# Sparse attention with a per-query search for the top 256 keys: visits of four key blocks, shorter search steps tied in order, and a memory pool of their own for selections and search buffers

## The chip, the cores and the metric

One Trainium2 chip, one of its cores. The metric is the time of the whole program on the device, in microseconds (us), as a median of runs. PE is TensorE (matmuls; its weight loads are shown as PEld), DVE is VectorE, ACT is ScalarE, POOL is GpSimd, SP is SyncE, which issues the DMAs.

## What is computed

One decoder layer on a prompt of 2048 tokens (and one new token for each of eight sequences with a cache of 4096 keys). The input projection feeds two groups of heads. One is RWKV-7 time mixing, a recurrence over the tokens. The other is sparse attention: an indexer scores every earlier key of a query, the 256 best keys are selected, and softmax attention runs over these alone. Both outputs go through one output projection.

```
s = relu(einsum('bqhd,bsd->bqhs', qi, kidx))          # 8 indexer heads
score = einsum('bqhs,bqh->bqs', s, wi)
score = where(arange(L)[None, :] <= qpos[:, None], score, -inf)
_, sel = top_k(score, 256)
k_sel, v_sel = gather_kv(sel)
logits = einsum('bqgrd,bqkgd->bqgrk', qg, k_sel) * HEAD_DIM ** -0.5   # 2 kv heads, 4 q heads each
p = softmax(where(valid, logits, -inf))
o = einsum('bqgrk,bqkgd->bqgrd', p, v_sel)
...
mix = concatenate([att, rw_out], -1) @ w_out
y = x + gate * mix
```

## The kernel before

The program has two phases. The first (`phase_g`) makes all projections and the RWKV heads. Its memory lies in pools stacked one behind the other on the left side of on-chip memory: `hp` holds the normalised input `h` (65,536 bytes per partition), `wp` four weight buffers `w` of 8,192 bytes and a staging buffer `wst` of 4,096, `bs` constants, and `bu` and `bv` the work buffers of the RWKV chunks, among them three `UA` buffers of 8,192 bytes. The last chunks of RWKV (`g_tail`) run after the last projection has read `h`; they end with a small chain on DVE and ACT (a norm, L796 to L814) and two transposes on PE (L810).

The second phase (`phase_a`) is attention over the 16 blocks of 128 queries, with L = 128 (i + 1) keys for block i. Its pools are stacked over the same memory: `ac` (constants, keys `K`, values `Vn`; 43.8 KB per partition), `aq` (query tiles `qT` and `qiT`, three score buffers `sc` of 8,192 bytes, the search's columns `sm`, the ReLU buffers `r`; 43.5 KB), and `ap` (everything else: the selections `bias`, three of 4,096 bytes, the search's buffer `t1` of 8,192, the probabilities `P`, `pT`, and small tiles). The pools are made with `reuse_waits="tile"`. The pools of the background work lie above `ap`.

Every block goes through three jobs:

- `scores(i)`: for each of 8 indexer heads, PE multiplies (L1031), ACT takes the ReLU (L1048), DVE adds it with the head's weight into `sc` (L1049). 8 turns for each 1024 keys.
- `search(i)`: finds a threshold for each query that leaves 256 keys. After a start from mean and square (L1069 to L1086), six steps of a bracketing method: ACT counts the keys above the trial value with Sign and an accumulated sum (L1092), and some twenty instructions on columns of 128 x 1 make the next trial value (L1093 to L1133). They run on POOL, for blocks 4 and 5 on DVE. At the end DVE and POOL make `t1` (L1137, L1138), DVE takes the eight largest (L1141) and writes the selection `bias`, 0 or a huge negative number for each key (L1144). Sign and Square write their unused result into a part of `bias`.
- `attend(i)`: for each of 4 pairs of heads, PE makes logits (L1031), DVE adds `bias` and takes the maximum (L1262), ACT takes the exponential (L1270). Then come the visits: for two key blocks at a time PE transposes the probabilities of both heads (L1279, 4 transposes, into one of two `t` banks), ACT copies them to `pT` (L1282), and PE multiplies them with the values (L1286, 4 products on tiles of 128 x 64).

Blocks are taken in the order 4, 15, 5, 14, 6, 13, 7, 12, 8, 11, 9, 10, 3, 2. In stage s, `merge` interleaves turn by turn the search of the stage's block, the attention of the block two stages back (in stage 3 also of blocks 0 and 1) and the scores of the next block, each in proportion to its stated number of turns. Every third turn it also advances the background: the decode tokens' work and, for blocks that are done, the output projection (`outproj`, L1342). The order in which the program emits instructions isn't yet the order on the engines: a scheduler orders each engine's instructions by their priority and its own estimate of time. `later(n)` shifts the priority: searches are moved ahead by 2000, the background back by 1500. On the chip each engine runs its instructions in that fixed order. `after(a, [b])` tells the scheduler to place `a` behind `b`, without a semaphore.

## Time and profile before

| | us |
|---|---|
| median of 3 runs | 2493.24 (2489.59 to 2494.8) |
| the profiled execution | 2486.81 |
| its span, first to last instruction | 2485.0 |
| PE busy | 2151.5 (87%) |
| DVE busy | 1603.3 (65%) |
| POOL busy | 1111.7 (45%) |
| ACT busy | 1056.2 (43%) |

The profile is of one execution. Busy times of PE include the time in which a slower clock was granted, and the ends of matmuls are modelled. In the rows, a tile's name stands for all its buffers, `out<-in` says what an instruction writes and reads, x is a count, and what follows `<-` in brackets is what ended the engine's idle time before it. Projections and RWKV take the first 1400 us, attention and the rest what remains; the two overlap for some 90 us.

### The profile page before, as it was taken

What the parts mean: (1) busy time and instruction counts of PE and PEld (TensorE: products, weight loads), DVE (VectorE), ACT (ScalarE), POOL (GpSimd) and SP (SyncE); (2) the same over time, 40 slices, a digit from 0 to 9 for tenths busy, and PEclk for the clock granted to TensorE, in tenths of its full rate; (3) what the DMA queues carried; (4) which work ended last, traced back from release to release, by engine and by line L of the source; (5) the groups of instructions that cost most, each with busy time, mean ns of one, the idle gap of its engine ahead of it and who ended that gap; (6) DMA issues with size and microseconds to landing.
All of it is one profiled execution on the core that took longest, in us unless ns stands there. A gap on an engine that the chain in (4) does not pass through costs nothing.

```text
span 2485.0 us, 57674 instructions
## 1 busy us (share of the span) xinstructions
PE 2151.5 (87%) x21559; PEld 1493.0 (60%) x21559; DVE 1603.3 (65%) x5101; ACT 1056.2 (43%) x2192; POOL 1111.7 (45%) x3369
## 2 busy tenths in 40 slices
PE   6778999599999999979999664898787898899997
PEld 2546777477778777867877431354444554555554
DVE  3873477477776566667777577766787754567421
ACT  1642233233333333322233245777776652665430
POOL 2311335233424234432334216447776774787712
PEclk9889999699999999999999775999998999999999
DMA  6434333321111211112211511322000032221233
GB/s 221 147 115 113 96 96 95 83 55 41 32 46 42 55 51 40 51 40 60 54 36 32 125 35 55 100 65 64 18 18 10 18 86 77 60 59 44 65 104 95
DMA packets 268196, 167.73 MB, mean 67 GB/s; under 512 B 108647, under 2 KB 240704, under 8 KB 267777
## 3 DMA queue, kind: packets, MB, share of 16 engines
q1 hardware_dynamic: 262465, 149.26, 21.6%
q0 software_dynamic: 3328, 10.49, 1.6%
q8 instruction: 171, 2.80, 0.5%
q10 hardware_dynamic: 2112, 4.19, 0.5%
q14 instruction: 120, 0.98, 0.1%
HBM read 113.87 MB, written 50.00 MB: 66 GB/s over the span
## 4 chain that ended last, share of the span: by engine, by line
PE 41%; POOL 22%; DMA 10%; DVE 9%; issue 8%; SPq 5%; ACT 4%; POOLq 0%; DVEq 0%; ACTq 0%
PE ps_g L196 10%; PE ps_s L1342 5%; PE ps_g L204 4%; PE ps_l L1031 3%; PE ps_v L1286 3%; PE ps_t L1279 3%; POOL Ut L652 2%; POOL Us L653 2%; SPq L644 2%; PE ps_e L619 2%; PE ps_g L159 2%; POOL sm L1123 1%; SPq L655 1%; ACT bias L1092 1%; DMA TT<-tsc 1%
## 5 line engine op out<-in xcount | busy, mean ns | idle before, releaser
L196 PE MATMUL ps_g<-h,w 128*128 128x256 f16 x4032 | 503.0, 279 | 13.1 <-ACT h L439 6.3
L196 PEld LDWEIGHTS <-w 128*128 128x128 f16 x4536 | 407.6, 100 | 93.4 <-issue 13.1
L652 POOL TENSOR_TENSOR Ut<-As,Us 128x12 f32<-128x12 f32 (+10 forms) x480 | 130.5, 272 | 282.8 <-DMA As<-asc 231.9
L204 PE MATMUL ps_g<-w,h 128*128 128x256 f16 (+1 forms) x2304 | 254.0, 264 | 0.3 <-ACT nat L849 0.2
L1262 DVE CUSTOM_DVE_ANT_0 P<-ps_l,bias 128x1024 f32<-128x1024 f32 (+7 forms) x192 | 172.0, 907 | 98.2 <-PE ps_l L1031 56.3
L204 PEld LDWEIGHTS <-h 128*128 128x128 f16 x2304 | 197.7, 99 | 30.7 <-issue 3.2
L1286 PE MATMUL ps_v<-pT,Vn 128*64 128x128 f32 x2176 | 185.8, 295 | 33.5 <-ACT pT L1282 33.2
L1049 DVE SCALAR_TENSOR_TENSOR sc<-r,wi,sc 128x1024 f32<-128x1024 f32 (+7 forms) x154 | 169.2, 1099 | 66.9 <-ACT r L1048 64.8
L1282 ACT COPY pT<-ps_t 128x512 f32<-128x512 f32 (+1 forms) x288 | 153.4, 559 | 130.1 <-PE ps_t L1279 129.7
L1279 PE MATMUL ps_t<-cf,P 128*128 128x128 f32 x1088 | 188.0, 296 | 15.4 <-ACT P L1270 15.0
L1270 ACT ACTIVATE P<-P,mx 128x1024 f32<-128x1024 f32 (+7 forms) x192 | 171.3, 895 | 53.1 <-DVE mx L1268 52.7
L1286 PEld LDWEIGHTS ps_v<-pT,Vn 128*64 128x64 f32 x2176 | 119.7, 141 | 114.8 <-ACT pT L1282 58.1
L1342 PE MATMUL ps_s<-wo,mt 128*128 128x512 f16 x768 | 173.8, 382 | 11.0 <-DVE sm L1142 7.6
L1031 PE MATMUL ps_l<-K,qT 128*128 128x512 f16 (+3 forms) x640 | 151.6, 359 | 23.2 <-ACT r L1048 16.3
L1092 ACT ACTIVATE bias<-sc,sm 128x640 uint8<-128x640 f32 (+13 forms) x84 | 109.7, 1307 | 143.7 <-POOL sm L1133 128.2
L1048 ACT ACTIVATE r<-ps_l 128x1024 f32<-128x1024 f32 (+7 forms) x176 | 141.4, 814 | 67.9 <-PE ps_l L1031 37.1
L1031 PE MATMUL ps_l<-K,qiT 128*128 128x512 f16 (+3 forms) x608 | 152.6, 377 | 18.8 <-DVE mx L1262 12.0
L1279 PEld LDWEIGHTS ps_t<-cf,P 128*128 128x128 f32 x1088 | 124.6, 147 | 69.0 <-issue 39.2
L653 POOL TENSOR_TENSOR Us<-Us,Ut 128x12 f32<-128x12 f32 (+10 forms) x480 | 132.1, 275 | 34.3
L1342 PEld LDWEIGHTS <-mt 128*128 128x128 f16 x768 | 75.2, 98 | 98.9 <-issue 15.2
L1031 PEld LDWEIGHTS <-qT 128*128 128x128 f16 x640 | 62.4, 101 | 79.9 <-issue 41.6
L1031 PEld LDWEIGHTS <-qiT 128*128 128x128 f16 x608 | 59.6, 105 | 82.2 <-issue 46.7
(584 smaller groups left out, 4284.0 us busy)
## 6 DMA issues: line engine op xcount, KB each, us to landing
xt<-in_xT SPq DMA_DIRECT2D x16, 512.0 KB
wa<-in_w_ada SPq DMA_DIRECT2D x8, 1024.0 KB
kxd<-pg SPq DMA_DIRECT2D x32, 256.0 KB
qTd<-qo SPq DMA_DIRECT2D x32, 256.0 KB
kx<-kxd SPq DMA_DIRECT2D x64, 128.0 KB
mt<-mixd SPq DMA_DIRECT2D x16, 512.0 KB
x<-in_x SPq DMA_DIRECT2D x32, 256.0 KB
out_y_p<-x SPq DMA_DIRECT2D x32, 256.0 KB
```

The lines of the kernel that those rows point to most:

```text
L196: self.PE.matmul(out, w[:, a, k], h[:, b, k], start=(n == 0), stop=(n == 3 * KD - 1))
L204: self.PE.matmul(out, h[:, b, k], w[:, a, k], start=(n == 0), stop=(n == 3 * KD - 1))
L652: G.tensor_tensor(Ut[:, 0:m, j + 1:], bc(As[:, j:j + 1, j + 1:], sh), bc(Us[:, 0:m, j:j + 1], sh), op=OP.mult)
L653: G.tensor_tensor(Us[:, 0:m, j + 1:], Us[:, 0:m, j + 1:], Ut[:, 0:m, j + 1:], op=OP.add)
L1031: self.PE.matmul(ps[:, j:j + m], qs, self.K[:, kk, c0 + j:c0 + j + m], start=st, stop=not st)
L1049: V.scalar_tensor_tensor(sc[:, c:c + n], r[:, :n], wi[:, h:h + 1], self.tz[:, c:c + n] if h == 0 else sc[:, c:c + n], op0=OP.mult, op1=OP. ...
L1262: V.tensor_tensor_reduce(P[n][:, :w], pl[:, :w], bias[:, c:c + w], scale=1.0, scalar=-3.0e38, op0=OP.add, op1=OP.max, accum_out=mx[:, h, n ...
L1270: A.activation(P[n][:, :w], P[n][:, :w], AF.Exp, scale=0.125, bias=mx[:, h, 2:3], accum_out=sums[:, n, h:h + 1])
L1279: PE.transpose(pt[:, q:q + 128], Ps[g][k // 8][:, k % 8 * 128:(k % 8 + 1) * 128], self.ident)
L1282: A.copy(pT[:, :w], pt[:, :w])
L1286: PE.matmul(pv[64 * g:64 * g + 64, hh * 128:(hh + 1) * 128], self.Vn[:, k, 64 * g:64 * g + 64], pT[:, q:q + 128], start=(k == 0), stop=(k ...
L1342: PE.matmul(pg, mt[:, b, k], self.wo[:, a, k, js], start=(n == 0), stop=(n == 3 * KD - 1))
```

## The change

Three things are done together.

- A new pool `as` stands between `ac` and `aq` and takes `bias` (3 x 4,096 bytes), `t1` (8,192) and `v8` (128) out of `ap`. `qT` (3 x 2,048) moves from `aq` to `ap`, and `pT` gets a fourth buffer.
- The search keeps its bracket with the sign turned, and its steps are written with fused instructions of two operations, whose operands may be columns: 13 instructions in the first step in place of 18, 16 in the next three in place of 22, 21 in the last two in place of 31; 11 ahead of the steps in place of 13, one new one behind them. Square, Sign and the instruction that makes `t1` are tied behind the latest large instruction of scores or attention that the program has emitted on the same engine.
- Attention visits four key blocks at a time: eight transposes into two banks, two copies, eight products, chained in order by ties and with the pair copied last taken first. The number of turns that `merge` counts for attention follows.

```
-                self.ac, self.aq, self.ap_ = apool("ac"), apool("aq"), apool("ap")
+                self.ac, self.as_, self.aq, self.ap_ = apool("ac"), apool("as"), apool("aq"), apool("ap")
...
-   jobs.append((chain(...), sum(4 * (4 + i // 2 + 1) for i in now), 0))
+   jobs.append((chain(...), sum(4 * (4 + i // 4 + 1) for i in now), 0))
...
-        self.qT[i] = self.aq.tile([128, 8, 128], F16, name="qT", bufs=3)
+        self.qT[i] = self.ap_.tile([128, 8, 128], F16, name="qT", bufs=3)
...
-        bias = ap.tile([128, T], BF16, name="bias", bufs=3)
+        t1 = self.as_.tile([128, T], F32, name="t1", bufs=1)
+        v8 = self.as_.tile([128, 16], F32, name="v8", bufs=2)
+        bias = self.as_.tile([128, T], BF16, name="bias", bufs=3)
...
-        A.activation(ja[:, :n1], sc[:, :n1], AF.Square, accum_out=col(1))
+        self.after(A.activation(ja[:, :n1], sc[:, :n1], AF.Square, accum_out=col(1)), [self.act])
...
-            A.activation(ja[:, :L], sc[:, :L], AF.Sign, scale=-1.0, bias=t, accum_out=col(5))
-            G.tensor_scalar(e, col(5), -0.5, L / 2 - 251.5, op0=OP.mult, op1=OP.add)
+            self.after(A.activation(ja[:, :L], sc[:, :L], AF.Sign, bias=t, accum_out=col(5)), [self.act])
+            G.tensor_scalar(e, col(5), 0.5, L / 2 - 251.5, op0=OP.mult, op1=OP.add)
             if k:
-                G.tensor_tensor(col(6), e, ep, op=OP.mult)
-                G.tensor_scalar(col(6), col(6), 0.0, -0.2, op0=OP.is_gt, op1=OP.mult)
-                G.tensor_tensor(m[:, 30:32], E[:, :, 1], bc(col(6), [128, 2]), op=OP.mult)
-                G.tensor_tensor(E[:, :, 1], E[:, :, 1], m[:, 30:32], op=OP.add)
+                G.tensor_scalar(col(6), e, ep, 0.0, op0=OP.mult, op1=OP.is_le)
+                G.tensor_scalar(le, col(6), 0.8, le, op0=OP.max, op1=OP.mult)
+                G.tensor_scalar(he, col(6), 0.8, he, op0=OP.max, op1=OP.mult)
...
-            G.tensor_tensor(tn, lt, col(16), op=OP.subtract)
-            G.tensor_tensor(col(25), e, e, op=OP.mult)
-            G.tensor_scalar(col(26), col(25), 13.0, None, op0=OP.is_gt)
-            G.tensor_scalar(col(25), col(25), 13.0, None, op0=OP.is_le)
-            G.tensor_tensor(tn, tn, col(26), op=OP.mult)
-            G.tensor_tensor(col(25), t, col(25), op=OP.mult)
-            G.tensor_tensor(tn, tn, col(25), op=OP.add)
+            G.tensor_scalar(col(16), col(16), lt, t, op0=OP.subtract, op1=OP.add)
+            G.tensor_scalar(col(25), e, e, 13.0, op0=OP.mult, op1=OP.is_le)
+            G.tensor_scalar(col(25), col(25), -1.0, col(16), op0=OP.add, op1=OP.mult)
+            G.tensor_scalar(tn, col(25), t, None, op0=OP.add)
...
-        t1 = ap.tile([128, T], F32, name="t1", bufs=1)
-        V.scalar_tensor_tensor(t1[:, :L], sc[:, :L], t, ..., accum_out=col(5))
+        self.after(V.scalar_tensor_tensor(t1[:, :L], sc[:, :L], t, ..., accum_out=col(5)), [self.dve])
...
-            for k0 in range(0, nk, 2):
-                kk = range(k0, min(k0 + 2, nk))
-                pt = self.bank("t", 2)
-                ... transposes of kk
-                pT = ap.tile([128, 512], F32, name="pT", bufs=3)
-                A.copy(pT[:, :w], pt[:, :w])
-                for k in kk:
-                    for g in range(2):
-                        PE.matmul(pv[...], self.Vn[:, k, ...], pT[:, q:q + 128], start=(k == 0), stop=(k == nk - 1), ...)
+            for k0 in range(0, nk, 4):
+                pTs = []
+                for k1 in range(k0, min(k0 + 4, nk), 2):
+                    kk = range(k1, min(k1 + 2, nk))
+                    pt = self.bank("t", 2)
+                    ... transposes of kk
+                    pT = ap.tile([128, 512], F32, name="pT", bufs=4)
+                    self.act = A.copy(pT[:, :w], pt[:, :w])
+                    pTs.append((kk, pT))
+                ks = [(k, (k - kk[0]) * 256, pT) for kk, pT in reversed(pTs) for k in kk]
+                for n, (k, q, pT) in enumerate(ks):
+                    for g in range(2):
+                        mm = PE.matmul(pv[...], self.Vn[:, k, ...], pT[...], start=(k0 == 0 and n == 0),
+                                       stop=(k0 + 4 >= nk and n == len(ks) - 1), ...)
+                        if n or g:
+                            self.after(mm, [last])
+                        last = mm
                 yield
```

`self.act` is set by the ReLU of `scores` and by the exponentials and copies of `attend`, `self.dve` by the weighted sum of `scores` and by the logits' maximum in `attend`. The steps 4 and 5 of the search lose four more instructions than the lines shown, in the same way.

## Rows read from the trace of the kernel before

**Rows 1.** The page's span in 40 equal slices of 62 us: busy share of PE and of POOL in tenths, and the granted clock of PE.
```profile
PE   6778999599999999979999664898787898899997
...
POOL 2311335233424234432334216447776774787712
PEclk9889999699999999999999775999998999999999
```
**Rows 2.** Busy time by stretches. Columns: the stretch, its length, then busy us (and instructions) of PE, PEld, DVE, ACT and POOL, then the granted clock, the DMA engines' share and GB/s.
```profile
1395.00:1490.00 95.00, 62.10 (x645) 35.88 (x645) 64.81 (x165) 39.26 (x62) 26.36 (x71) 0.77 0.25 53
1490.00:1540.00 50.00, 16.30 (x54) 4.49 (x54) 39.95 (x339) 24.91 (x41) 33.26 (x128) 0.50 0.18 51
1540.00:1600.00 60.00, 53.56 (x339) 22.66 (x339) 45.15 (x94) 43.01 (x79) 29.90 (x73) 0.94 0.27 78
1600.00:2360.00 760.00, 664.77 (x5016) 389.74 (x5016) 493.59 (x1241) 480.65 (x888) 532.48 (x1788) 0.95 0.18 51
2360.00:2485.00 125.00, 112.27 (x687) 58.98 (x685) 29.79 (x88) 25.18 (x61) 22.47 (x18) 0.98 0.36 100
```
**Rows 3.** What PE waited for from 1400 us to the end: us in total, times, the longest.
```profile
PE ps_v L1286 <- ACT pT L1282: 33.2, 25, 3.0
PE ps_l L1031 <- ACT r L1048: 22.9, 28, 3.3
PE ps_s L1425 <- DVE sm L1133: 22.4, 1, 22.4
...
PE ps_t L1279 <- ACT P L1270: 15.0, 9, 3.1
```
**Rows 4.** ACT's timeline at the end of the RWKV tail: start us, length us, instruction. L803 reads `UA`, L1069 is the Square of a search (640 columns: block 4; 1024: block 15).
```profile
1486.01 0.42 ACT L803 ACTIVATE Y<-UA 128x256 f32<-128x256 f32 x1 [7.10 <-DVE UA L800]
1486.34 0.72 ACT L1069 ACTIVATE bias<-sc 128x640 uint8<-128x640 f32 x1
...
1487.05 1.04 ACT L1069 ACTIVATE bias<-sc 128x1024 uint8<-128x1024 f32 x1
```
**Rows 5.** DVE's timeline: the last addition to the scores of block 4 and the search's first instruction on its columns, the last addition to the scores of block 15, and its selection.
```profile
1421.04 0.88 DVE L1049 SCALAR_TENSOR_TENSOR sc<-r,wi,sc 128x640 f32<-128x640 f32 x1
...
1421.97 0.15 DVE L1071 TENSOR_SCALAR sm<-sm 128x1 f32<-128x1 f32 x1
...
1458.81 1.24 DVE L1049 SCALAR_TENSOR_TENSOR sc<-r,wi,sc 128x1024 f32<-128x1024 f32 x1
...
1573.50 3.32 DVE L1144 SCALAR_TENSOR_TENSOR bias<-sc,sm,pw 128x2048 bf16<-128x2048 f32 x1
```
**Rows 6.** PE's timeline: the last product of the RWKV tail and the next instruction.
```profile
1490.08 0.66 PE L810 MATMUL ps_s<-cf,UA 128*128 128x128 f32 x2 [5.08 <-DVE UA L807]
1513.19 1.10 PE L1425 MATMUL ps_s<-cf,sdu 8*128 8x8 f32 x9 [22.45 <-DVE sm L1133]
```
**Rows 7.** Groups of instructions by line, from 1395 us on: count, then busy us and mean ns of one, then idle time before them. The copies of the visits, and the logits' products.
```profile
L1282 ACT COPY pT<-ps_t 128x512 f32<-128x512 f32 (+1 forms) x288 | 153.4, 559 | 130.1 <-PE ps_t L1279 129.7
...
L1031 PE MATMUL ps_l<-K,qT 128*128 128x512 f16 (+3 forms) x640 | 151.6, 359 | 23.2 <-ACT r L1048 16.3 <-DVE mx L1262 6.5
```
**Rows 8.** POOL's timeline of one step of a search, which nothing disturbs: the first two of its 22 instructions, the power, and the last.
```profile
2042.17 0.19 POOL L1093 TENSOR_SCALAR sm<-sm 128x1 f32<-128x1 f32 x1 [0.56 <-ACT bias L1092]
2042.45 0.19 POOL L1096 TENSOR_TENSOR sm<-sm 128x1 f32<-128x1 f32 x1
...
2045.75 0.57 POOL L1123 TENSOR_TENSOR sm<-sm,pw 128x1 f32<-128x1 f32 x1
...
2047.36 0.19 POOL L1133 TENSOR_TENSOR sm<-sm 128x1 f32<-128x1 f32 x1
```
**Rows 9.** What ACT waited for from 1400 us to the end: us in total, times, the longest.
```profile
ACT bias L1092 <- POOL sm L1133: 128.2, 50, 8.5
ACT P L1270 <- DVE mx L1268: 52.7, 27, 10.9
```
**Rows 10.** The timeline of all engines around one Sign.
```profile
1687.89 1.28 DVE L1049 SCALAR_TENSOR_TENSOR sc<-r,wi,sc 128x1024 f32<-128x1024 f32 x1
1688.04 1.18 POOL L1126 TENSOR_TENSOR sm<-sm 128x1 f32<-128x1 f32 x1
...
1689.79 1.04 ACT L1092 ACTIVATE bias<-sc,sm 128x896 uint8<-128x896 f32 x1 [3.11 <-POOL sm L1133]
...
1690.83 1.05 ACT L1282 COPY pT<-ps_t 128x512 f32<-128x512 f32 x2
...
1691.45 1.12 PE L1286 MATMUL ps_v<-pT,Vn 128*64 128x128 f32 x8 [2.88 <-ACT pT L1282]
```
**Rows 11.** PE's weight loads (PEld) in attention where nothing is awaited: value products (L1286), transposes (L1279), and at the end the product of the scores (L1031).
```profile
1666.16 0.42 PEld L1279 LDWEIGHTS ps_t<-cf,P 128*128 128x128 f32 x4 [0.17 <-issue]
1666.74 0.42 PEld L1286 LDWEIGHTS ps_v<-pT,Vn 128*64 128x64 f32 x8 [0.17 <-ACT P L1270]
1667.33 0.42 PEld L1279 LDWEIGHTS ps_t<-cf,P 128*128 128x128 f32 x4 [0.17 <-issue]
1667.92 0.42 PEld L1286 LDWEIGHTS ps_v<-pT,Vn 128*64 128x64 f32 x8 [0.17 <-issue]
1668.51 0.42 PEld L1279 LDWEIGHTS ps_t<-cf,P 128*128 128x128 f32 x4 [0.17 <-issue]
1668.89 0.10 PEld L1031 LDWEIGHTS <-qiT 128*128 128x128 f16 x1
```

More of the change, by code (lines that the diff above doesn't have):

```diff
@@ L951, in phase_a @@
                     if now:
-                        jobs.append((chain(*(self.attend(i) for i in now)), sum(4 * (4 + i // 2 + 1) for i in now), 0))
+                        jobs.append((chain(*(self.attend(i) for i in now)), sum(4 * (4 + i // 4 + 1) for i in now), 0))
                     if s == A01 - 1:
@@ L1104, in search @@
+            G.tensor_scalar(col(21), e, 0.0, None, op0=OP.is_le)
             w = m[:, 32:36].rearrange("p (a b) -> p a b", a=2)
[L1105 to L1106 removed]
+            G.tensor_tensor(w, bc(m[:, None, c:c + 2], [128, 2, 2]), E, op=OP.subtract)
+            G.tensor_tensor(w, w, bc(m[:, 20:22, None], [128, 2, 2]), op=OP.mult)
@@ L1119, in search @@
+                G.tensor_scalar(lt, col(23), L * 2.0 ** -126, lt, op0=OP.max, op1=OP.min)
+                G.tensor_scalar(ht, col(23), -1.0, ht, op0=OP.mult, op1=OP.max)
             G.tensor_tensor(m[:, 16:18], E[:, 0], E[:, 1], op=OP.subtract)
@@ L1181, in bisect @@
         sc = self.sc[i]
-        bias = ap.tile([128, T], BF16, name="bias", bufs=3)
+        bias = self.as_.tile([128, T], BF16, name="bias", bufs=3)
         self.bias[i] = bias
@@ L1261, in attend @@
                     P.append(ap.tile([128, 1024], F32, name="P", tag="P", bufs=PB))
-                    V.tensor_tensor_reduce(P[n][:, :w], pl[:, :w], bias[:, c:c + w], scale=1.0, scalar=-3.0e38,
+                    self.dve = V.tensor_tensor_reduce(P[n][:, :w], pl[:, :w], bias[:, c:c + w], scale=1.0, scalar=-3.0e38,
                                            op0=OP.add, op1=OP.max, accum_out=mx[:, h, n:n + 1])
@@ L1269, in attend @@
                 for n, (c, w) in enumerate(ch):
-                    A.activation(P[n][:, :w], P[n][:, :w], AF.Exp, scale=0.125, bias=mx[:, h, 2:3], accum_out=sums[:, n, h:h + 1])
+                    self.act = A.activation(P[n][:, :w], P[n][:, :w], AF.Exp, scale=0.125, bias=mx[:, h, 2:3], accum_out=sums[:, n, h:h + 1])
                 Ps.append(P)
                 yield
-            for k0 in range(0, nk, 2):
-                kk = range(k0, min(k0 + 2, nk))
-                pt = self.bank("t", 2)
-                for k in kk:
-                    for g in range(2):
-                        q = ((k - k0) * 2 + g) * 128
-                        PE.transpose(pt[:, q:q + 128], Ps[g][k // 8][:, k % 8 * 128:(k % 8 + 1) * 128], self.ident)
-                w = 256 * len(kk)
-                pT = ap.tile([128, 512], F32, name="pT", bufs=3)
-                A.copy(pT[:, :w], pt[:, :w])
-                for k in kk:
-                    for g in range(2):
-                        q = ((k - k0) * 2 + g) * 128
-                        PE.matmul(pv[64 * g:64 * g + 64, hh * 128:(hh + 1) * 128], self.Vn[:, k, 64 * g:64 * g + 64], pT[:, q:q + 128],
-                                  start=(k == 0), stop=(k == nk - 1), tile_position=(0, 64 * g))
@@ new lines, in attend @@
+            for k0 in range(0, nk, 4):
[3 more added lines that the diff above has]
+                    pt = self.bank("t", 2)
+                    for k in kk:
+                        for g in range(2):
+                            q = ((k - k1) * 2 + g) * 128
+                            PE.transpose(pt[:, q:q + 128], Ps[g][k // 8][:, k % 8 * 128:(k % 8 + 1) * 128], self.ident)
+                    w = 256 * len(kk)
+                    pT = ap.tile([128, 512], F32, name="pT", bufs=4)
[3 more added lines that the diff above has]
+                for n, (k, q, pT) in enumerate(ks):
+                    for g in range(2):
+                        mm = PE.matmul(pv[64 * g:64 * g + 64, hh * 128:(hh + 1) * 128], self.Vn[:, k, 64 * g:64 * g + 64],
+                                       pT[:, q + g * 128:q + g * 128 + 128], start=(k0 == 0 and n == 0),
+                                       stop=(k0 + 4 >= nk and n == len(ks) - 1), tile_position=(0, 64 * g))
+                        if n or g:
+                            self.after(mm, [last])
+                        last = mm
```

48 lines of the change are left out of this document (18 added, 30 removed).

## The prediction

> **What bounds the kernel now.** I read the page's forty slices first. TensorE (PE) is nearly always busy until slice 23, drops to 6, 6, 4 of ten in the three slices that end the projections and open attention, with its clock falling too, and then stays between 6 and 9 [rows 1]. Next the table by stretches [rows 2]: from 1395 us on PE is idle for 95 - 62.10 = 32.9, 50 - 16.30 = 33.7, 60 - 53.56 = 6.4, 760 - 664.77 = 95.2 and 125 - 112.27 = 12.7 us, together 181 us of 1090. So PE sets the end, nearly at its limit in the tail of output projections, and what can be won is its idle time, its slow clock (0.50 of full from 1490 to 1540, the 1.2 GHz level) and work that it needn't do. Then who ends PE's waits [rows 3]: one wait of 22.4 us, and 33.2 + 22.9 + 15.0 = 71.1 us for ScalarE (ACT). Two faults, then: an empty changeover, and ACT late in attention.
>
> **The pool over the projections' memory.** Per partition, h has 65,536 bytes, the four w buffers 32,768, staging 4,096; behind them lie bs and bu, whose UA buffers the RWKV tail reads to its end. Before, ac (43.8 KB) and aq (43.5 KB) come first, so ap, with the selections (bias) and t1, begins 87.3 KB in and reaches over w, bs and bu. After, the new pool (8,192 + 128 + 12,288 bytes) lies from 43.8 to 64.4 KB, inside h, which is dead once the last projection is done. The trace shows what the old place costs: the scores of block 4 are complete at 1421.9, yet ACT's first search instruction (Square, which writes into bias) starts at 1486.34, straight behind ACT's last read of UA at 1486.01, and that of block 15 with it at 1487.05 [rows 4, 5]. PE ends the tail at 1490.7 and has nothing until 1513.19 [rows 6].
> Gain: attention of the first large block, 15, needs its selection, written at 1573.50 + 3.32 = 1576.8 [rows 5]; its search took 1576.8 - 1487.05 = 89.8 us. Its scores end at 1458.81 + 1.24 = 1460.05 [rows 5]. Started there, and 10.8 us shorter (next part), it ends at about 1539, 38 us earlier. PE has to do meanwhile what it did from 1490 to 1577: 16.3 us at half clock, 8 at full, and 37 x 53.56 / 60 = 33, so 41 us from 1491, to 1532 [rows 2]: not later than the search. I take **-38**. Bounds: -22, the one wait alone [rows 3], and -55, idle time and slow clock of 1490 to 1600 (33.7 + 8 + 6.4) and a fifth of what lies before. What hides it is VectorE (DVE): it is busy 64.81 of 95 us in the tail [rows 2], and the search of block 4 (on DVE) now runs there; without that cover its 115 instructions push the tail out by up to 115 x 0.15 = 17 us (0.15 us is a search instruction on DVE [rows 5]), which the -22 leaves room for.
> What moves the other way: qT goes from aq to ap, so the logits of block 4's first two heads, computed ahead before, and SyncE's loads of qT must now follow each engine's last use of bu. Two heads are eight matmuls of 0.36 us [rows 7]: **+3**. The loads come behind the tail's last TT transfers on SP's queue; those end well ahead of PE's last tail product, which needs them, and PE can't use qT before that, so nothing is later for it.
>
> **Shorter steps.** A search step on POOL has 18 instructions at k = 0, 22 at k = 1 to 3 and 31 at k = 4, 5: 146. After: 13, 16 and 21: 103. The opening falls from 13 to 11, one sign flip comes at the end: 159 to 115. An undisturbed step of 22 runs from 2042.17 to 2047.55, 0.245 us each [rows 8]; 44 fewer are 10.8 us a search. Twelve of fourteen searches run on POOL. Where it counts: Sign stands in ACT's queue until the last POOL instruction is done; ACT lost 128.2 us in 50 such waits, 2.56 each [rows 9]. PE pays when copies for it stand behind the Sign: ACT waits 3.11 us, copies after, and PE has waited 2.88 us for them [rows 10]. POOL's share of what makes ACT late is 128.2 / (128.2 + 52.7) = 0.71 [rows 9] (ACT's waits for PE are effects), so 0.71 x 71.1 = 50 us of PE's idle time. A step loses 43 / 6 x 0.245 = 1.76 of the 2.56 us, 69%: 35 us, of which I take **-30**, since a shorter step lets ACT meet fewer instructions in between. Bounds: the fused form with two operands from columns isn't in the trace. The nearest rows are the two-operation form with constants, 0.19 us, and the power, 0.57 [rows 8]. At 0.57 for the eight in a step it would lose 8 x 0.38 - 6 x 0.245 = 1.6 us instead of winning 1.5: +30. I go by 0.19, the same opcode. Upper end -71, all of PE's waits for ACT.
> A POOL instruction also stretches from 0.19 to 1.18 us until a DVE instruction with two inputs ends [rows 10]; I leave those stalls as they are.
> **The ties** (no semaphore, only order) forbid that a Sign stands ahead of a ReLU, exponential or copy issued earlier in the program, and t1 ahead of DVE's last logits. Behind a tied Sign wait only the search's own steps, and their user is attention two stages later: no cost while a search ends a stage early. They can only shorten what copies wait behind a Sign; it is inside the bounds above.
>
> **Visits of four key blocks.** Transposes (t) and value products (v) alternate. With nothing awaited, v and t runs start 0.58 to 0.59 us apart though the array loads for 0.42, while the score product behind a t run comes 0.38 us after it [rows 11]: each change between t (128 x 128) and v (128 x 64 tiles) leaves 0.17 us empty, 0.34 a visit. Visits: 4 heads x 72 = 288, as many as copies [rows 7]; in fours 4 x 40 = 160. 128 x 0.34 = 43.5 us. PE is busy 718 of 820 us from 1540 to 2360 [rows 2], so 0.88 of it counts, and I let a quarter go where other products split a longer run: **-29**. Bounds 0 and -44.
> The Trainium skill (TensorE: Matmul & The Clock Gate, Step-by-step: what each phase is for) says that the drain of one matmul overlaps the filling of the next, so back to back only the columns count. By that the changes are free and the sum would be 29 us less. The trace disagrees: 0.17 us at each [rows 11]. It agrees with another page (TensorEngine Tiling (Array Packing), Key Properties): changing the tiling mode drains the engine.
> What it adds: the first v now waits for the second of two copies (reversed order). Two copies back to back take 1.05 us [rows 10], bare where PE has no other product. Before, 25 of 288 runs waited [rows 3, 7]. I take ten more waits of that length, **+10**; bounds 0 and 160 x 1.05 = +168.
> At no cost: one more pT buffer, the weight in the interleaving, background pools 2 KB higher.
>
> **Sum.** -38 + 3 - 30 - 29 + 10 = -84. The profiled execution took 2486.81 (span 2485.0): 2403. The median is 6.4 above it: **2409**.
>
> **Rivals.**
> 1. Only the changeover pays: PE's output projections fill what ACT leaves, and later waits merely move. For it: PE is 0.88 busy. Against: 95 us idle in spite of the filler. 2493 - 35 = 2458.
> 2. The searches don't start earlier (something but memory holds Square back): 84 - 35 = 49 won, 2444. Against it, three Squares released at once behind UA's reader.
> 3. The changes of tiling are free (the first page above says so): 2409 + 29 = 2438. The rows speak against it.
> 4. The changeover and the visits reach their lower bounds and PE's waits for ACT shrink by 60 of 71 us: -55 + 3 - 60 - 44 = -156, 2337.
> 5. Slower: the copies lie bare. Each visit now has two copies between its transposes and its products, two t banks hold just one visit, so the next visit's transposes can't run ahead of the copies, and PE waits when no score product is ready. It decides from 94 / 160 = 0.6 us a visit on; at 0.85 in each it costs 136 us against 94 won: 2535. For it: ACT is 63% busy in attention and in order. Against: only 33.2 us of such waits now.
>
> **How the numbers follow.** Forecast 0.50; rival 1 0.16, rival 2 0.06, rival 3 0.04, rival 4 0.10, rival 5 0.12, and 0.02 that it evens out. About 0.2% (5 us) is what a measurement here can tell. Faster 0.86, same 0.02, slower 0.12. Range: 2335, just past rival 4, to 2475 (the -22 alone gives 2471, and the runs shown spread by 5); rival 5 is left out.
>
> **What would show it.** Square of block 4 near 1425 and PE's 22 us wait gone; clock above 0.8 from 1490 to 1540; the selection of 15 near 1540. POOL steps of 16 instructions in about 3.9 us; ACT's waits for POOL under 60 us. PE's v runs of 16 loads, t runs of 8, and PE's wait for pT not above 45 us. It is wrong if v's waits for pT exceed 95 us, if fused POOL instructions take over 0.4 us, or if the RWKV tail ends after 1505.

## The result and the profile after

The changed kernel takes 2522.9 us (median of 4 runs, 2517.1 to 2529.0), the kernel before 2492.75 in the same comparison: a ratio of 1.0125, 95% interval 1.0101 to 1.0149. It is slower; the forecast was 2409, and its range ended at 2475. The profiled execution has a span of 2526.7 us against 2485.0, 41.7 more. Of these, 1412.5 - 1401.6 = 10.9 lie ahead of the first score product, where PE runs the same products in the same order and the granted clock is 0.922 in the mean against 0.937: some 31 us belong to attention.

The busy time by stretches, as [rows 2] (same columns):

```profile
1395.00:1490.00 95.00, 60.84 (x617) 35.46 (x614) 65.36 (x184) 43.08 (x70) 37.08 (x94) 0.79 0.30 69
1490.00:1540.00 50.00, 23.46 (x143) 12.77 (x143) 34.25 (x161) 23.84 (x37) 36.35 (x95) 0.53 0.10 29
1540.00:1600.00 60.00, 47.43 (x289) 23.79 (x286) 52.46 (x163) 37.24 (x77) 19.28 (x31) 0.83 0.23 67
1600.00:2360.00 760.00, 642.48 (x5009) 391.76 (x5007) 480.95 (x1253) 491.68 (x912) 522.28 (x1288) 0.94 0.18 51
2360.00:2526.80 166.80, 131.87 (x752) 66.41 (x749) 39.87 (x109) 16.27 (x41) 33.39 (x43) 0.94 0.33 91
sum 1131.80, PE 906.08 PEld 530.19 DVE 672.89 ACT 612.10 POOL 648.39; mean PE 181.22 PEld 106.04 DVE 134.58 ACT 122.42 POOL 129.68
```

PE is busy 906.1 us from 1395 us to the end, 909.0 before, and idle 1131.8 - 906.1 = 225.7 us against 181. (The near-equal busy times hide less work at a slower clock; the table under "What is shown" takes the two apart.) Until 1600 us nothing is won (73.3 idle, 73.0 before; the clock from 1490 to 1540 is 0.53, still near the 1.2 GHz level). From 1600 to 2360 the idle time is 117.5 against 95.2, in the last stretch 34.9 against 12.7.

What PE waited for from 1395 us on, as [rows 3]:

```profile
PE ps_l L1032 <- ACT r L1049: 44.9, 40, 7.0
PE ps_l L1032 <- DVE mx L1253: 23.3, 18, 3.1
PE ps_v L1282 <- ACT pT L1277: 19.7, 17, 5.0
PE ps_t L1274 <- ACT pT L1277: 17.1, 16, 4.7
PE ps_s L1342 <- DVE t L1346: 13.6, 15, 1.8
PE ps_s L810 <- DVE sm L1097: 10.1, 1, 10.1
PE ps_t L1274 <- ACT P L1261: 9.9, 7, 4.0
```

The single wait of 22.4 us is gone, as forecast. In its place the last products of the RWKV tail (L810) wait 10.1 us for DVE, 5.1 in [rows 6]; PE waits 44.9 us for ReLU instead of 22.9, and there is a wait that was only 0.3 us before: transposes for copies of pT, 17.1. The row of L810 names a search instruction (sm L1097), the last that DVE ran before it; what L810 reads is written by L807, just ahead of that.

The changeover, as [rows 4 to 6]: the timeline of ACT (L1072 Square, L1093 Sign, L803 of the tail), then that of the other engines (L1094 a search, L796 the tail's reduction, L1480 key scores of the background, L1347 the end of an output projection, L1296 a block's attention done), then three lines of the kernel before for the last three.

```profile
1432.89 0.74 ACT L1072 ACTIVATE bias<-sc 128x640 uint8<-128x640 f32 x1
...
1503.15 2.00 ACT L1093 ACTIVATE bias<-sc,sm 128x2048 uint8<-128x2048 f32 x1 [4.95 <-POOL sm L1124]
...
1508.71 0.42 ACT L803 ACTIVATE Y<-UA 128x256 f32<-128x256 f32 x1 [2.65 <-DVE UA L800]
```
```profile
1506.09 0.15 DVE L1094 TENSOR_SCALAR sm<-sm 128x1 f32<-128x1 f32 x1 [3.71 <-ACT bias L1093]
...
1507.48 0.42 DVE L796 TENSOR_REDUCE gx<-ps_m 128x4 f32<-128x256 f32 x1
...
1514.42 0.66 PE L810 MATMUL ps_s<-cf,UA 128*128 128x128 f32 x2 [10.12 <-DVE sm L1097]
...
1558.71 2.33 DVE L1135 SCALAR_TENSOR_TENSOR bias<-sc,sm,pw 128x2048 bf16<-128x2048 f32 x1
...
1573.55 1.05 PE L1480 MATMUL ps_s<-kx,qiT_s 64*32 64x512 f32 x4
...
2119.34 1.27 POOL L1347 TENSOR_TENSOR x<-x,t 128x512 f32<-128x512 f32 x1
...
2395.36 0.28 DVE L1296 COPY rT<-ps_t 8x128 f32<-8x128 f32 x1 [1.23 <-PE ps_t L1294]
```
```profile
1519.02 2.96 PE L1480 MATMUL ps_s<-kx,qiT_s 64*32 64x512 f32 x8 [0.28 <-DVE swt L1443]
...
2026.04 1.27 POOL L1347 TENSOR_TENSOR x<-x,t 128x512 f32<-128x512 f32 x1
...
2443.59 0.28 DVE L1296 COPY rT<-ps_t 8x128 f32<-8x128 f32 x1 [6.48 <-PE ps_t L1294]
```

The Square of block 4 starts at 1432.89, before the tail's end; the searches stand among the tail's instructions. How that holds the tail can be read off its end: a Sign of block 15 waits 4.95 us on ACT for POOL, the Sign of block 4 stands behind it, DVE's next instruction (L1094, the search of block 4) waits 3.71 us for that Sign, and the tail's reduction (L796) comes behind it at 1507.48, 3.5 us after the last product that it reads is done (L783, 1503.96); in the kernel before it came 0.05 us after that. The tail ends at 1515.1, 24.3 later than in [rows 6], 13.5 of it counted from the first score product. The selection of 15 is done at 1561.0, 16 us earlier than in [rows 5], or 27 counted from the first score product, not 38: its Square starts at 1470.0 and the search takes 91.0 us, where the prediction had 1460 and 79. Then look at the background, PE's filler: its first key scores (L1480) start at 1573.55 and its first output projection ends at 2120.6, where the trace of before has 1519.0 and 2027.3. The last block's attention is over at 2395.4, 48 us earlier than before (2443.6), and the end comes 131 us behind it, where before it came 41 behind: when the last value product is done, 384 of the 768 products of the output projections are still to come, 124 in the kernel before.

One step of a search on POOL, as [rows 8], the shortest of those with 16 instructions:

```profile
1903.98 0.19 POOL L1094 TENSOR_SCALAR sm<-sm 128x1 f32<-128x1 f32 x1 [1.83 <-ACT bias L1093]
1904.27 0.31 POOL L1097 TENSOR_SCALAR sm<-sm 128x1 f32<-128x1 f32 x1
...
1905.43 0.30 POOL L1098 TENSOR_SCALAR sm<-sm 128x1 f32<-128x1 f32 x1
...
1907.86 0.34 POOL L1119 TENSOR_SCALAR sm<-sm 128x1 f32<-128x1 f32 x1
1908.31 0.38 POOL L1121 TENSOR_SCALAR sm<-sm 128x1 f32<-128x1 f32 x1
...
1909.16 0.29 POOL L1124 TENSOR_SCALAR sm<-sm 128x1 f32<-128x1 f32 x1
```

It runs from 1903.98 to 1909.45: 5.47 us, against 5.38 for the 22 instructions of [rows 8]. The instructions that take operands from columns last 0.27 to 0.38 us and start 0.27 to 0.48 apart. Six fewer instructions save nothing; nor do they over the steps with nothing else of POOL's among them, 6.2 us in the median before (19 steps of 22 instructions) and 6.4 after (25 of 16).

### The profile page after: what moved, and what is told of

It reads as the page before. It is cut to its first block, busy times and chain, and to the rows that moved or that the text cites. A ratio compares the mean times of both kernels' runs of the same rounds, so it can differ in the third digit from the quotient of the medians.

```text
span 2526.7 us, 56947 instructions
## 1 busy us (share of the span) xinstructions
PE 2156.4 (85%) x21559; PEld 1514.9 (60%) x21559; DVE 1596.6 (63%) x5013; ACT 1054.0 (42%) x2192; POOL 1113.1 (44%) x2841
## 5 line engine op out<-in xcount | busy, mean ns | idle before, releaser
L196 PE MATMUL ps_g<-h,w 128*128 128x256 f16 x4032 | 511.4, 282 | 14.6 <-ACT h L439 6.3
L1274 PE MATMUL ps_t<-cf,P 128*128 128x128 f32 x1088 | 184.5, 297 | 28.7 <-ACT pT L1277 17.1
L1050 DVE SCALAR_TENSOR_TENSOR sc<-r,wi,sc 128x1024 f32<-128x1024 f32 (+7 forms) x154 | 162.8, 1057 | 72.1 <-ACT r L1049 71.2
L1032 PE MATMUL ps_l<-K,qiT 128*128 128x512 f16 (+3 forms) x608 | 160.5, 388 | 47.2 <-ACT r L1049 33.0
L1277 ACT COPY pT<-ps_t 128x512 f32<-128x512 f32 (+1 forms) x288 | 152.6, 559 | 113.7 <-PE ps_t L1274 103.5
L1282 PE MATMUL ps_v<-pT,Vn 128*64 128x128 f32 x2176 | 162.7, 292 | 22.6 <-ACT pT L1277 19.7
L1274 PEld LDWEIGHTS ps_t<-cf,P 128*128 128x128 f32 x1088 | 130.4, 149 | 80.4 <-issue 27.1
L1032 PE MATMUL ps_l<-K,qT 128*128 128x512 f16 (+3 forms) x640 | 159.0, 373 | 21.7 <-ACT r L1049 11.8
L1093 ACT ACTIVATE bias<-sc,sm 128x640 uint8<-128x640 f32 (+13 forms) x84 | 109.9, 1309 | 115.1 <-POOL sm L1124 103.9
L653 POOL TENSOR_TENSOR Us<-Us,Ut 128x12 f32<-128x12 f32 (+10 forms) x480 | 126.5, 264 | 34.4
```

The lines of the kernel that those rows point to most:

```text
L196: self.PE.matmul(out, w[:, a, k], h[:, b, k], start=(n == 0), stop=(n == 3 * KD - 1))
L1032: self.PE.matmul(ps[:, j:j + m], qs, self.K[:, kk, c0 + j:c0 + j + m], start=st, stop=not st)
L1050: self.dve = V.scalar_tensor_tensor(sc[:, c:c + n], r[:, :n], wi[:, h:h + 1], self.tz[:, c:c + n] if h == 0 else sc[:, c:c + n], op0=OP.mu ...
L1093: self.after(A.activation(ja[:, :L], sc[:, :L], AF.Sign, bias=t, accum_out=col(5)), [self.act])
L1274: PE.transpose(pt[:, q:q + 128], Ps[g][k // 8][:, k % 8 * 128:(k % 8 + 1) * 128], self.ident)
L1277: self.act = A.copy(pT[:, :w], pt[:, :w])
```

## The experiments

Theories. **A**: the visits of four take 128 turns from the merge (838 to 710), the background advances once in three turns, so PE's filler comes late. **B**: the early searches delay the RWKV tail and with it the filler. **C**: each edit makes the planner lay out another order of the same instructions, and the order moves the time by more than the parts do. The table has the median, the ratio to the kernel before on the same chip (2487 to 2493 us there) with its 95% interval, and of the profiled execution PE's busy and idle time from 1395 us to the end.

| kernel | us | ratio | busy | idle |
|---|---|---|---|---|
| before | 2492.8 | | 909.0 | 181.0 |
| before_bg1400 | 2491.8 | 1.0001 [0.9983, 1.0020] | 916.9 | 181.4 |
| before_bg1000 | 2509.0 | 1.0064 [1.0039, 1.0089] | 912.2 | 205.8 |
| pace_before | 2509.9 | 1.0069 [1.0046, 1.0092] | 910.8 | 196.6 |
| before_short | 2518.2 | 1.0086 [1.0057, 1.0115] | 933.5 | 190.0 |
| before_pool | 2520.3 | 1.0103 [1.0071, 1.0134] | 931.8 | 191.2 |
| pool_tailtie | 2519.3 | 1.0124 [1.0096, 1.0151] | 929.2 | 193.6 |
| before_fours | 2514.7 | 1.0092 [1.0058, 1.0127] | 900.6 | 216.7 |
| before_fours_pace | 2510.9 | 1.0097 [1.0062, 1.0133] | 888.0 | 220.9 |
| fours_dve | 2551.5 | 1.0260 [1.0238, 1.0283] | 911.1 | 239.5 |
| after_twos | 2512.4 | 1.0087 [1.0055, 1.0118] | 924.4 | 188.5 |
| twos_bg1000 | 2498.4 | 1.0049 [1.0028, 1.0069] | 924.6 | 183.9 |
| twos_tailtie | 2512.9 | 1.0099 [1.0071, 1.0126] | 928.5 | 195.8 |
| after | 2522.9 | 1.0125 [1.0101, 1.0149] | 906.1 | 225.7 |
| after_noties | 2524.2 | 1.0157 [1.0134, 1.0180] | 907.2 | 218.5 |
| after_tailfirst | 2523.2 | 1.0114 [1.0081, 1.0147] | 908.2 | 223.9 |
| pace_after | 2502.9 | 1.0051 [1.0027, 1.0075] | 895.8 | 208.0 |
| pace_after_bg500 | 2504.9 | 1.0054 [1.0033, 1.0074] | 902.6 | 212.7 |
| after_bg1000 | 2499.3 | 1.0031 [1.0010, 1.0052] | 893.6 | 205.5 |
| after_tailtie | 2480.7 | 0.9962 [0.9941, 0.9983] | 898.5 | 184.7 |

**The pace of the background.** The same edit, with the old ratio of steps to turns in the kernel after and the new one in the kernel before:

```
-            if tick % BGT == 0:
+            self.owed += 838              # pace_before: 710
+            if self.owed >= 3 * 710:      # pace_before: 3 * 838
+                self.owed -= 3 * 710
```

> The kernel after, with one thing changed: the background (loading and use of the output weights, the single-token path, the output projections) advances one step per 2.54 turns of the merge instead of per 3, so that the 710 turns that are left of 838 carry as many background steps as before. Theory A (the visits of four took 128 turns out of the merge, so the background, PE's filler, came later; output projections begin at 2119 us instead of 2026 and 45 us more of PE's idle time stay unfilled): output projections begin near 2030 again, PE's idle time from 1395 us on falls from 226 towards 181, and the time falls to about 2480. Theory B (the searches that now stand among the last RWKV instructions push that tail out by 24 us, and attention never wins it back): the tail still ends near 1515 and the time stays at 2515 to 2525.

> The kernel before, with one thing changed: the background advances one step per 3.54 turns instead of per 3, which is the pace that the kernel after has. Theory A: output projections begin some 90 us later, PE's idle time grows by 20 to 45 us, and the time is 2515 to 2540. Theory B: the pace is free, 2490 to 2498.

Both came out on A's side: 20 us less in the kernel after, 0.7% more in the kernel before. But by its own markers A is only half right: output projections begin at 2086 (not 2030), and in the kernel before at their old place but for one block, which comes at 1734. The pace isn't free, and it isn't the whole loss: 0.5% stay.

**One part at a time on the kernel before, and the change without its visits.**

```
before_fours, _pace: for k0 in range(0, nk, 4): ... (attention of after), weight 4 + i // 4 + 1
before_pool:  self.ac, self.as_, self.aq, self.ap_ = ...; bias, t1, v8 in as_, qT in ap_
before_short: the body of search() of after, without ties, tiles where they were
after_twos:   for k0 in range(0, nk, 2): ... (attention of before), weight 4 + i // 2 + 1
```

> The kernel after without the visits of four: attention's inner loop and its weight in the merge as before, with the pool over h, the shorter steps and the ties as after. Theory A: the 128 turns are back, output projections begin near 2030, and what the changeover and the short steps win shows: 2435 to 2480. Theory B: the tail of RWKV still ends near 1515; 2500 to 2525, more than after by PE's 23 us in the value products at most. If the visits of four themselves are what costs (new waits for the second copy), it is also near 2470, but then the kernel before with visits of four is slower than 2520.

> The kernel before with the visits of four alone: the loop over four key blocks, its order and its weight in the merge (128 turns fewer), no ties, no new pool, long steps. Theory A: the background comes later as in the kernel after; PE's value products fall by some 23 us and its unfilled time grows by more: 2495 to 2520. Theory B: the visits are a gain by themselves: 2465 to 2480.

> The kernel before with the visits of four and the background's pace restored (one step per 2.54 turns). Tells the pace of the visits from the visits themselves, whose run without the pace took 24 us more than before. If the lost turns are what costs there: 2475 to 2492, the value products' gain. If the visits cost by themselves (PE's transposes now wait for the copies that hold both t banks: 21 us of such waits there, 0.3 before): 2500 to 2512, with those waits again near 20 us.

> The kernel before with the pool alone: selections, t1 and v8 over h, qT in ap; long steps, no ties, visits of two. If the pool is what delays the RWKV tail and the background (first instructions of the searches in front of them): the tail ends some 13 us later than in the kernel before, counted from the first score product, the background's key scores begin near 1560 instead of 1519 us, and the time is 2505 to 2520. If the changeover gains as predicted and the ties or steps cost: 2455 to 2475.

> The kernel before with the shorter steps alone, memory, visits and order left as they are, no ties. As predicted (30 us of PE's idle time won): 2460 to 2475. If PE's waits for ACT merely move, or the background on POOL and DVE is what counts: 2485 to 2495. If fewer POOL instructions shift the background, which stands 1500 places of priority behind, to a later time: 2495 to 2510.

Every part alone costs 0.9 to 1.0%, all three together 1.25%: the costs don't add. before_pool comes out as its first branch has it: the selection of 15 is done at 1548.5, but the tail ends 105.3 us after the first score product (89.1 in the kernel before), key scores begin at 1564.9 and output projections at 2109. after_twos speaks against A: it has its 128 turns back, and still output projections begin at 2099, with the tail 103.5 us after the first score product. PE's waits of before_fours, as [rows 3]:

```profile
PE ps_v L1289 <- ACT pT L1284: 39.3, 19, 5.4
...
PE ps_t L1281 <- ACT pT L1284: 21.5, 12, 4.1
PE ps_l L1031 <- ACT r L1048: 19.1, 27, 2.2
```

The waits for copies are 60.8 us, 33.5 before (v 33.2, t 0.3). PE is busy 8 us less and idle 36 more; with the pace restored it is 21 and 40. So the visits' gain is there and is given back as idle time, with or without the lost turns. In before_short the two instructions of POOL with two operands from columns (count, busy, mean ns, idle), and ACT's wait for it, as [rows 9]:

```profile
L1118 POOL TENSOR_SCALAR sm<-sm 128x1 f32<-128x1 f32 x72 | 34.6, 481 | 6.8
L1116 POOL TENSOR_SCALAR sm<-sm 128x1 f32<-128x1 f32 x72 | 34.2, 475 | 6.7
```
```profile
ACT bias L1090 <- POOL sm L1121: 141.3, 50, 7.1
```

With everything else as before, the short steps leave ACT waiting 141.3 us, in 50 waits again, against 128.2. Neither the tail (88.9 us from the first score product to its end, 89.1 before) nor the background is late there (first output projection at 2030); still the time is 0.9% up. That is nothing that A or B can explain.

**Controls: only the place of the background.**

```
-P_BG, P_SE, BGT = 1500, -2000, 3
+P_BG, P_SE, BGT = 1400, -2000, 3      # 1000, 500
```

> A control: the kernel before, with the background 1400 instead of 1500 places behind in the planner's order and nothing else (some 2% of PE's instructions stand elsewhere, no part of the change is in it). If what costs is what each part does: 2485 to 2497, no difference. If the kernel before is a lucky order and any other order of the same work costs some 20 us (theory C): 2505 to 2520.

> A larger control: the kernel before with the background 1000 places behind instead of 1500. Theory A says that an earlier filler can't hurt: 2470 to 2495. Theory C: 2505 to 2520, the same size as every other edit.

> The kernel after with the background 1000 places behind instead of 1500. Theory A (the filler comes too late): output projections begin earlier than 2119 us and 2495 to 2512. Theory C: 2505 to 2530 without a trend.

> The kernel after with the pace restored (one step per 2.54 turns, 2503 us in its run) and the background 500 places behind instead of 1500. Theory A: still less than that, 2470 to 2498, output projections beginning before 2060 us. If the background's own chain (key scores, then the search over all pages) sets when output projections can begin, and not its place in the order: 2495 to 2510.

A small nudge changes nothing. A larger one, the same direction and size in both kernels, costs the kernel before 0.6% and brings the kernel after 24 us. This doesn't refute A: a nearer place in the planner's order isn't an earlier filler on the chip. In the kernel before, output projections then begin at 2046 instead of 2026, 20 us later; in the kernel after at 2081 instead of 2119, 38 earlier; and each time goes the way of its filler. What the two show is that the same shift suits the one kernel and not the other. In pace_after_bg500 a place of 500 adds nothing to the restored pace (2504.9 against 2502.9): output projections begin at 2090, not before 2060, as its second branch has it. What A can't explain are before_short and after_twos, above.

**What holds the copies, and what the ties do.**

```
 fours_dve:      if k1 == k0: A.copy(pT, pt)
                 else:        V.tensor_copy(pT, pt)
 after_noties:   Square, Sign and t1 without self.after(...)
```

> The kernel before with visits of four and the pace restored (2511 us, PE's waits for pT 40.2 + 17.3 us), and the second copy of each visit made by VectorE instead of ScalarE, so that the two t banks come free side by side. If the bare copies are what eats the 26 us that PE saves in the value products: these waits fall below 35 us and the time to 2485 to 2500. If it is the order of the work around them: 2503 to 2515.

> The kernel after without the ties: Square, Sign and t1 may stand ahead of ReLU, exponential, copy and logits that were issued earlier in the program. If the ties keep waits for POOL out of the copies' way, as they are meant to: ScalarE's waits for POOL rise from 112 to 130 us or more and the time to 2525 to 2540. If they cost (searches end later, PE's waits for ReLU 44.9 us): these waits fall below 35 us and 2500 to 2515. Within 5 us of 2523 they do neither.

PE's waits of fours_dve:

```profile
PE ps_l L1034 <- ACT r L1051: 44.4, 35, 4.5
PE ps_t L1284 <- ACT pT L1288: 35.4, 24, 4.5
```

With half of the copies on DVE, waits for pT fall little (45.5 us with those for DVE's, from 57.2), those of the transposes double, and the time is the worst of all. The test failed: the copies moved to VectorE cost time themselves or by their order (output projections begin at 2116 there, at 2045 in before_fours_pace), so it doesn't separate the copies from the order. The ties change nothing in the time. Without them ACT's waits for POOL rise (126.2 us, 103.9 with them) and PE's waits for copies of pT with them (55.5 us, 36.8), but PE's idle time as a whole doesn't (218.5, 225.7).

**The first searches behind the tail.** after_tailfirst takes away the searches' lead of 2000 places for blocks 4 and 15:

> The kernel after, with one thing changed: the searches of blocks 4 and 15 aren't raised by 2000 places in the order, so that they stand behind the RWKV tail's last instructions where both are ready. If it is the raised searches that push the tail out: from the first score product to the tail's end 89 to 93 us instead of 102.6, and 2500 to 2515, 8 to 20 less than after. If the tail is late for another reason (fewer free buffers, DVE's rate): no change, 2518 to 2528.

The order on PE and on ACT stayed the same and so did the time (2523.2 and 2522.9): place numbers don't decide there. Why not, no run shows; the planner may put a ready search into every gap of the tail. after_tailtie forces it:

```
+        self.tlv = V.scalar_tensor_tensor(yc, yc, ...)    # end of the tail
+        self.tla = A.copy(ym[:, 0], yc)
-        self.after(A.activation(... AF.Square ...), [self.act])
+        self.after(A.activation(... AF.Square ...), [self.act] + ([self.tla] if i in (4, 15) else []))
+        if i == 4: self.after(first, [self.tlv])          # first DVE instruction of the search
```

> The kernel after, with the first ScalarE instruction of the searches of blocks 4 and 15 and the first VectorE instruction of that of block 4 held behind the RWKV tail's last ones on the same engine (order only). If the searches among the tail's instructions delay it and with it all that follows: the tail ends 89 to 93 us after the first score product instead of 102, the background's key scores begin near 1530 and the time is 2500 to 2515. If the tail's delay is paid back by the earlier selections: the selection of 15 comes later by 15 to 25 us and the time is 2518 to 2535.

It is faster than both kernels, 0.4% below before on the same chip and 42 us below after. Busy time by stretches, then the timeline:

```profile
1395.00:1490.00 95.00, 63.18 (x668) 37.93 (x667) 65.21 (x157) 35.60 (x56) 26.11 (x68) 0.77 0.24 51
1490.00:1540.00 50.00, 21.46 (x68) 6.78 (x68) 30.90 (x162) 23.88 (x38) 29.88 (x87) 0.50 0.24 69
...
1600.00:2360.00 760.00, 656.83 (x5083) 401.38 (x5081) 505.60 (x1309) 487.70 (x899) 527.65 (x1301) 0.94 0.19 53
2360.00:2478.16 118.16, 104.71 (x645) 55.99 (x642) 31.39 (x91) 25.02 (x61) 29.36 (x44) 0.97 0.35 97
```
```profile
1493.76 0.66 PE L810 MATMUL ps_s<-cf,UA 128*128 128x128 f32 x2 [4.87 <-DVE UA L807]
...
1520.72 4.02 PE L1482 MATMUL ps_s<-kx,qiT_s 64*32 64x512 f32 x8 [0.64 <-DMA kx<-kxd]
...
1578.93 2.35 DVE L1137 SCALAR_TENSOR_TENSOR bias<-sc,sm,pw 128x2048 bf16<-128x2048 f32 x1
...
2034.78 1.27 POOL L1349 TENSOR_TENSOR x<-x,t 128x512 f32<-128x512 f32 x1 [2.06 <-DVE t L1348]
...
2430.74 0.28 DVE L1298 COPY rT<-ps_t 8x128 f32<-8x128 f32 x1 [0.52 <-PE ps_t L1296]
```

The tail ends as before (87.5 us after the first score product), the background starts at 1520.7, output projections at 2035, and 123 of their products are left when the last value product is done. The selection of block 15 comes at 1581.3, 20 us later than in the kernel after and later than in the kernel before, attention ends at 2431 instead of 2395, and the whole is 42 us shorter. So the time doesn't hang on that selection. The same tie on two neighbours, before_pool (there for block 5 too) and after_twos, and after_twos with the background at 1000:

> The kernel before with the pool alone (2520 us), and the searches of blocks 4, 15 and 5 held behind the RWKV tail's last ScalarE and VectorE instructions. If the early searches are all that the pool costs: the tail ends 88 to 91 us after the first score product instead of 105, key scores of the background begin near 1525, and the time is 2485 to 2497, as before. If the place of the memory costs in another way: 2505 to 2520.

> The kernel after with the tail's order (2481 us) and without the visits of four. If the visits gain there (PE's value products cost 16 to 26 us less, waits for pT are 28.8 us in that run): 2488 to 2505. If they still cost: 2460 to 2476.

> The kernel after without the visits of four (2512 us) and with the background 1000 places behind instead of 1500, which gave the kernel after 24 us back. If pool and short steps gain what was predicted once the filler is in place: 2430 to 2465. If they only move waits: 2485 to 2505.

pool_tailtie has the tail and the start of the background all but in place, from the first score product 88.0 and 116.1 us (89.1 and 117.4 in the kernel before). Its first output projection comes 17 us later than there (641.1, 624.4), and its attention ends 18 us later (1059.9, 1042.0):

```profile
1497.49 0.66 PE L810 MATMUL ps_s<-cf,UA 128*128 128x128 f32 x2 [4.87 <-DVE UA L807]
...
1526.26 3.43 PE L1484 MATMUL ps_s<-kx,qiT_s 64*32 64x512 f32 x8 [0.89 <-DVE sm L1129]
...
2051.26 1.27 POOL L1351 TENSOR_TENSOR x<-x,t 128x512 f32<-128x512 f32 x1
...
2470.08 0.28 DVE L1300 COPY rT<-ps_t 8x128 f32<-8x128 f32 x1 [6.48 <-PE ps_t L1298]
```

It is 1.2% slower, as before_pool was. twos_tailtie, whose tail (90.7 us) and first output projection (616.3) are as early as in the kernel before, is no better than after_twos either. So the tie brings the tail back in three kernels and the time in one: B, too, isn't enough. twos_bg1000 missed the forecast's gain (2430 to 2465) and lies where waits merely move.

## Why the prediction was wrong, step by step

1. **The changeover (-38).** Nothing of it reached the end. The memory did what was said: the Square moved up, PE's 22.4 us wait went. But the search was no shorter (91.0 us, 89.8 before), and everything stood 10.9 us later in this execution, so the selection came 16 us earlier (27 without the late start), not 38; the tail was pushed out by 13.5 us, inside the 17 that the prediction allowed; and the background, which I hadn't followed at all, began 55 us later. The step that failed is "attention of the first large block, 15, needs its selection", read as if the end needed it. after_tailtie shows that it doesn't: a selection 20 us later, an end 42 us earlier. What moved with the end in these two is PE's filler: output projections that begin 85 us earlier, and 41 us less of PE's idle time (184.7, 225.7). What I called a bound, "not later than the search", compared two chains and left out the third.
2. **Shorter steps (-30).** Mis-sized to nothing. The term rested on 0.19 us for the fused form; it takes 0.27 to 0.38 undisturbed, and 0.475 or 0.481 in the mean with two operands from columns (before_short). A step of 16 takes 5.47 us and one of 22 took 5.38. The upper bound, no gain and up to 30 us lost, was the better guide. ACT's waits for POOL came to 103.9 us, not under 60, and PE's for ACT, which this term was to shorten, grew: 91.6 us for ReLU, copies and exponentials (44.9 + 19.7 + 17.1 + 9.9), 71.4 before. What the runs show instead is that fusing two operations saves instructions and no time on POOL.
3. **Visits of four (-29, +10).** The first size was near, in part by luck: PE's value products are busy 162.7 us, 185.8 in the trace of before, 23.1 less where 29 were forecast, and the transposes 184.5 and 188.0, 3.5 less. That is 0.21 us for each of the 128 visits saved, where I read 0.34 off [rows 11]; the discounts for split runs and for PE's idle time made up for it. It speaks against rival 3: the changes of tiling aren't free. Rival 3 rests on the Trainium skill (TensorE: Matmul & The Clock Gate, Step-by-step: what each phase is for), by which the drain of one matmul overlaps the fill of the next. But with visits alone idle time grew by 36 us, of which the copies' waits are 27: +10 was too little, inside its bound of 168.
4. **"At no cost: ... the weight in the interleaving".** Wrong by itself: pace_before costs 0.7%, pace_after returns 20 us.
5. **The ties (nothing)** came out as said, by after_noties. **qT (+3)** was never run by itself; no wait of PE for a load of qT shows in the traces of after and before_pool.
6. **Rivals.** The time fell near rival 5, 2535, but not by its mechanism: waits for pT in the kernel after are 36.8 us, 33.5 before. Of the marks of failure the RWKV tail's end came true (1515.1, mark 1505; without the late start it would be 1504.2, at the mark), and that of the fused instructions (0.4 us) in their means only. Of the marks of success the early Square, the wait of 22 us and PE's wait for pT (36.8, mark 45) held; the clock from 1490 to 1540 (0.53, mark 0.8), the selection of 15 (1561, mark 1540) and a step's length (5.47, mark 3.9) didn't. What rival 1 says, that later waits merely move, describes the kernels best, but the level to which they return isn't that of before.

**What is shown and what isn't.** Shown: the instructions of the kernel after, in other orders of the same work, take from 2481 to 2524 us (after, after_noties, the two paces, after_bg1000, after_tailtie), those of the kernel before 2491 to 2510. These are the few orders that were tried, no full bands, but they overlap; the kernel before lies at the low end of its own, the kernel after at the high end. So what the change's work is worth, 23 us of PE's value products among it, can't be told from what the order does, and order alone gives back all that was lost and 0.4% more. That is C, with a limit: a small shift (before_bg1400) does nothing. The lead of 0.4% isn't one of work over work either: the tie was not tried on the kernel before by itself.

What the loss consists of can be read for each kernel by splitting PE's busy time since the first score product by the granted clock of its trace, 2.4 or 1.2 GHz. The column "at full clock" counts what ran at 1.2 GHz half. That is an estimate; it is borne out by the first five rows, which have visits of two and come to the same work within 3 us. The other kernels with visits of two come to 842.9 to 854.4 (the high ones are before_pool, after_twos and twos_bg1000), so it is good to some 10 us.

| kernel | busy | of it at 1.2 GHz | at full clock | idle |
|---|---|---|---|---|
| before | 902.8 | 114.4 | 845.6 | 180.6 |
| before_bg1400 | 913.1 | 136.5 | 844.8 | 181.1 |
| before_short | 921.4 | 157.8 | 842.5 | 189.5 |
| pool_tailtie | 915.2 | 144.0 | 843.2 | 192.4 |
| twos_tailtie | 918.1 | 148.7 | 843.7 | 195.2 |
| before_fours | 893.9 | 151.4 | 818.2 | 216.3 |
| after | 891.5 | 139.3 | 821.8 | 222.8 |
| after_tailtie | 887.1 | 129.6 | 822.3 | 184.2 |

The visits of four do save 23 to 27 us of PE's work. In before_fours and after the slow clock takes 12 to 19 of them back (half of the difference in the third column) and the idle time another 36 to 42; in after_tailtie it is 8 and 4. Open: what makes an order good. Late filler is part of it (after_tailtie, pace_after), but before_short and twos_tailtie have early filler, pool_tailtie's is only 17 us late, and all three are slow. There 15 to 22 us of the loss are the slow clock and 9 to 15 idle time, in many waits of 1 to 8 us (PE for ReLU 33.3, 38.0 and 33.7 us, 22.9 before). It isn't the one profiled execution: in the mean of their runs the granted clock is 0.917 to 0.920, in the runs of before beside them 0.923 to 0.924. Why PE works more at the slow clock in these orders no run shows.

## What to carry to other kernels

Where a planner lays out the order, an edit is two changes: the work and a new order. Before believing the sign of a difference under 2%, run the old and the new work in two or three other orders; if the bands overlap, the edit hasn't shown anything. To bring a chain forward pays only if the end waits for it: follow the filler that fills the idle time, too, and try to hold the newcomer behind a chain that it would split: that tie brought this kernel 42 us, and its two neighbours nothing. Compare PE's busy times only together with the granted clock.

## What the runs showed that was not expected

On POOL fewer instructions aren't less time: a tensor-scalar instruction on one column takes 0.19 to 0.24 us with constants, 0.27 to 0.31 with one operand from a column, 0.34 to 0.38 with two, and a tensor-tensor instruction on the same shapes 0.19 to 0.20. From start to start a step's instructions are now 5.47 / 16 = 0.34 us apart, 0.245 before [rows 8]. And PE's busy time: the same PE work was busy 909 us in one profiled execution of the kernel before and 917 in that of before_bg1400, whose time is the same. The difference is the clock, 114.4 and 136.5 us at 1.2 GHz: the profiled execution of the kernel before had a granted clock of 0.927 over its span, that of before_bg1400 0.919, and the runs of both 0.923 in the mean.
